# A hybrid attention block on one core: the first 256 channels in tiles of 128, the root in column form

## Chip, cores and metric

One core of a Trainium2 chip runs the whole block in one launch. The metric is device time in microseconds of one execution, as the median of several runs; a profile of one execution gives its span, from the first to the last instruction.

## The reference

One layer over 512 latent tokens and 256 context tokens of width 2048. Both streams are normalised and modulated, projected by one matrix, and pass through two groups of four heads (gated linear attention and mLSTM, in both directions); then an output projection, a convolutional SwiGLU and a final norm. What matters here is its beginning:

```python
mod = (c_act @ w_mod + b_mod)[:, None, :]         # c_act = silu(c)
mod_c = (cc_act @ w_mod + b_mod)[None, None, :]   # cc_act = silu(c_ctx)
sh1, sc1, gt1, sh2, sc2, gt2 = jnp.split(mod, 6, axis=-1)
csh1, csc1, cgt1, csh2, csc2, cgt2 = jnp.split(mod_c, 6, axis=-1)
h  = rmsnorm(x, g_norm1) * (1 + sc1) + sh1        # x: 512 tokens x 2048
hc = rmsnorm(ctx, g_norm1) * (1 + csc1) + csh1    # ctx: 256 tokens x 2048
z  = jnp.einsum('btd,dp->btp', h, w_in)           # q, k, v, gates of all heads
```

`rmsnorm` divides each token by the root of the mean square of its 2048 channels. All arrays are float32.

## The kernel before, in words

Tokens lie along the free dimension and channels on the 128 partitions, so x is sixteen tiles `xl[k]` of 128 channels x 512 tokens; the context is `xc[k]`, 128 x 256, two to a transfer (`xcp`). Every product of activations and weights is made in three passes: each operand is split into a high part (ACT rounds it) and a low part (DVE subtracts), and `mm3` adds high x high, high x low and low x high. `load_split` fetches a 512 KB piece of weights, two channel tiles by 512 columns (q 128, k 128, v 256 of one head), and splits it.

The head of the program is `project_first` (line 411). Its TensorE instructions are pinned: `mm` and `tr` keep them in the order in which they are written. It projects heads 0 and 1, pair of channel tiles by pair (`kp`, eight of them). Head 0 has six accumulators that stay in PSUM for all pairs (`banks`, groups g: 0 is q, 1 is k, 2 and 3 are v of the latent, 4 and 5 are k and v of the context). Head 1 is made one pair at a time in two other banks (`early_group`) and added to sums in SBUF.

Ahead of the first product stand:

- 16 transfers of x on SP's queue, and with each of the first 14 a filler product into an idle bank (line 418), whose result nothing uses.
- `stream_rstd` (line 539): ACT squares each tile, DVE adds the sixteen squares to one, and TensorE multiplies by ones, which gives every partition the sum of a token's squares; `mean_rsqrt` then makes the root on all 128 x 512 elements (`rl`).
- `mod_load`, `mod_rows`, `mod_cols` (lines 273 to 309), for region 1 (scale) and region 0 (shift) and 256 channels each: four pieces of 512 KB are fetched, sixteen products with the activated conditioning (`cact`) as the stationary side give rows, ACT copies them, two transposes and a reduction on DVE turn them into columns `scol` and `shcol`.
- `modulate(n, streams)` (line 562), for two channel tiles: DVE multiplies x by scale and root, ACT adds the shift into the high part `hTh`, DVE makes the low part `hTl`.

The same steps for later pairs are laid between products, so that their waits run under them. The context is squared, summed, rooted (`ss_c`) and modulated after the first products of head 1; `shifted` leaves h itself in the tiles of x for a later product. In the loop over `kp`, head 1's six groups come first, then head 0's, with the rows of the next pairs among them.

Two things set the order of the rest: instructions under `tc.high_priority()` go ahead of others on their engine, and `tc.issue_after(ins)` keeps a block's instructions behind one. SP issues transfers in program order, and one that has to wait for a buffer holds back those behind it. The buffers named `raw` are seven for scale and shift (`mraw`) and four for weights (`wraw`); the fourth piece of every scale or shift load goes into `wraw`. PSUM has six banks for accumulators (`acc`) and two for the rest (`psb`).

Of the kernel before, what the change touches and what calls it, by code (L numbers as in the profile page):

```python
# [11 lines left out]
F32 = mybir.dt.float32  # L12
F32R = mybir.dt.float32r
# [5 lines left out]
P = 128  # L19
# [65 lines left out]
def block_kernel(ctx: ExitStack, tc: tile.TileContext, a: dict, out: bass.AP):  # L85
# [25 lines left out]
    def mm(*args, **kw):  # L111
        ins = PE.matmul(*args, **kw)  # L112
        if pinned[0]:
            tc.keep_in_program_order(ins)
# [43 lines left out]
    def acc(name, shape=(P, T)):  # L158
        return (banks8[0] if banks8 else psA).tile(list(shape), F32, name=name, tag="acc")
# [113 lines left out]
    def mod_load(region, n):  # L273

        raws = []
        for q in range(4):
            raws.append((wraw if q == 3 else mraw).tile([P, 4, 256], F32, name=f"raw_m{region}_{n}_{q}", tag="raw"))
            nc.sync.dma_start(raws[q], a["w_mod1"][8 * region + n, q])
        return raws

    def mod_rows(region, n, raws):

        bank = psb(f"ps_m{region}_{n}")
        ps = bank[:, 0:256]
        for q in range(4):
            for g in range(4):
                mm(ps[32 * g : 32 * g + 32, :], cact[:, 4 * q + g, :], raws[q][:, g, :],
                   start=(q == 0), stop=(q == 3), skip_group_check=True)
        rows = tmp.tile([P, 256], F32, name=f"rows_m{region}_{n}", tag="rows")
        with tc.high_priority():  # L290
            S.copy(rows, ps)
        return bank, rows
# [115 lines left out]

    early_both = []

    def project_first():

        banks = [acc(f"a0_{g}", BANKS[g]) for g in range(6)]
# [12 lines left out]
        with tc.high_priority():  # L426
            ins = modulate(0, "x")

        for _ in range(6):
            mm(banks[5][:, 0:P], ones, rl[:, 0:P], start=True, stop=True)  # L430
        early_pair(w1, sums)
        for g in range(2, 4):
            early_group(0, g, w1, sums)
        project_chunk(0, *w0, banks[0], 0)
        rows = mod_rows(1, 1, raws[1])
        project_chunk(0, *w0, banks[1], 1)
        mod_cols(1, 1, *rows)
        with tc.high_priority(), tc.issue_after(ins):
            stream_rstd([x.rearrange("p a b -> p (a b)") for x in xcp], rc, "c", TC)
            ins = modulate(0, "c")  # L440
        for g in range(2, 4):
            project_chunk(0, *w0, banks[g], g)
        rows = mod_rows(0, 1, raws[0])
        early_group(0, 4, w1, sums)
        mod_cols(0, 1, *rows)
        early_group(0, 5, w1, sums)
        with tc.issue_after(ins):
            modulate(1, "xc")
        w1 = load_split(a["w_heads"][1, 1], f"h1_1")
        for r in (1, 0):  # L450
            raws[r] = mod_load(r, 2)
        nc.sync.dma_start(cst[:, 0:C_ID], a["consts"][:, 0:C_ID])
        project_chunk(0, *w0, banks[4], 4)
        rows = mod_rows(1, 2, raws[1])
        project_chunk(0, *w0, banks[5], 5)
        mod_cols(1, 2, *rows)
        shifted(0)
        for kp in range(1, KP):
            for g in range(6):
                if g == 5 and kp + 1 < KP:  # L460
                    rows = mod_rows(0, kp + 1, raws[0])
                ins = early_group(kp, g, w1, sums)
                if g == 2:
                    with tc.issue_after(ins):
                        w0 = load_split(a["w_heads"][0, kp], f"h0_{kp}")
                    if kp + 2 < KP:
                        raws[1] = mod_load(1, kp + 2)
            if kp + 1 < KP:
                mod_cols(0, kp + 1, *rows)
                with tc.issue_after(ins):  # L470
                    modulate(kp + 1, "xc")
# [47 lines left out]
    rstd = xp.tile([P, T + TC], F32, name="rstd")  # L519

    nc.sync.dma_start(cv, a["cvec"])
    xl = [ytile(k, f"xl{k}") for k in range(KT)]
    xcp = [actp.tile([P, 2, TC], F32, name=f"xc{j}", tag=f"al{KT // 2 + j}") for j in range(KT // 2)]
    xc = [xcp[k // 2][:, k % 2, :] for k in range(KT)]
    for k in range(KT):
        nc.sync.dma_start(xl[k], a["xT"][k])
    nc.sync.dma_start(cst[:, C_ID : C_LO + 2], a["consts"][:, C_ID : C_LO + 2])
# [8 lines left out]

    V.tensor_scalar(out=bp1, in0=bmod[:, 16:32], scalar1=1.0, scalar2=None, op0=ALU.add)

    def stream_rstd(xs, o, name, n):

        tot = xp.tile([P, T], F32, name=f"sq_{name}", tag="sqs")
        for k, x in enumerate(xs):
            if k == 0:
                sq = tot
            elif len(xs) == KT:
                tag = f"ah{1 + k}" if k < 11 else f"al{k - 9}"
                sq = actp.tile([P, T], F32, name=f"sq_{name}{k}", tag=tag)
            else:
                sq = tmp.tile([P, T], F32, name=f"sq_{name}{k}", tag="sq")
            S.activation(sq, x, AF.Square)  # L550
            if k:
                add(tot, tot, sq)
        ps = psb(f"ss_{name}", (P, n))
# [4 lines left out]
        mean_rsqrt(ps, D, var, scr, o)  # L558

    rl, rc = rstd[:, 0:T], rstd[:, T:]  # L560

    def modulate(n, streams):
        def part(x, r, k, c, hi, lo):
            S.activation(hi, x, AF.Identity, bias=shcol[:, k, c : c + 1])
            return V.scalar_tensor_tensor(out=lo, in0=x, scalar=shcol[:, k, c : c + 1], in1=hi.bitcast(F32), op0=ALU.add,
                                          op1=ALU.subtract).ins

        ks = (2 * n, 2 * n + 1)
        for k in ks:
            if "x" in streams:  # L570
                V.scalar_tensor_tensor(out=xl[k], in0=xl[k], scalar=scol[:, k, 0:1], in1=rl, op0=ALU.mult, op1=ALU.mult)
            if "c" in streams:
                V.scalar_tensor_tensor(out=xc[k], in0=xc[k], scalar=scol[:, k, 1:2], in1=rc, op0=ALU.mult, op1=ALU.mult)
# [911 lines left out]
def arrange(x, c, ctx, c_ctx, w_mod, b_mod, g_norm1, g_norm2, w_in, gla_w_lr, gla_b_lr, mlstm_b_gate,  # L1485
# [18 lines left out]
    r["xT"] = x[0].T.reshape(KT, P, T)  # L1504
    r["ctxT"] = ctx[0].T.reshape(KT // 2, 2, P, TC).transpose(0, 2, 1, 3)
    r["w_mod1"] = w_mod[0][:, : 2 * D].reshape(4, 4, P, 16, 256).transpose(3, 0, 2, 1, 4)
    r["w_mod2"] = w_mod[0][:, 2 * D :].T.reshape(4, KT, P, 2, 2, T).transpose(3, 0, 1, 2, 4, 5)
    small = np.concatenate([w_in[:, GLA_COLS["lr"] : GLA_COLS["lr"] + 16], w_in[:, ML_COLS["lr"] : ML_COLS["lr"] + 16]], 1)
    r["w_small"] = small.reshape(KT, P, 32).transpose(1, 0, 2)
# [43 lines left out]
```

## Time and profile before

| | us |
|---|---|
| median of 3 runs | 2439.01 (2438.06 to 2441.04) |
| the profiled execution | 2438.32 |
| its span | 2436.3 |
| TensorE busy | 2410.7 (99%) |
| VectorE busy | 1784.9 (73%) |
| ScalarE busy | 1016.7 (42%) |

The profile gives busy time by engine and by group of instructions, a timeline in which neighbouring instructions of a kind are merged, and for each idle stretch the engine or transfer that ended it. PE is TensorE's products and PEld its weight loads. A float32 product that isn't split into parts runs as two passes, and each pass has a record of its own. A product's record includes its latency, so records overlap: the pace of a series is read from the distance of its starts.

### The profile page before, as it was taken

Reading aid. Unit: us, or ns where it says so; the run is one execution under the profiler, and the core shown is the slowest. Engines: PE = TensorE matmul, PEld = TensorE weight load, DVE = VectorE, ACT = ScalarE, POOL = GpSimd, SP = SyncE. Lnnn points to the kernel's source line nnn. Section 1 sums busy time; section 2 is a strip of 40 time slices with the busy share of each in tenths; the row PEclk is TensorE's granted clock in tenths of the full one; section 3 lists DMA queues with packets and bytes.
Section 4 is the critical chain, followed back from the end, with each engine's and each line's share of the span. In section 5 each row is a group of like instructions: output and inputs, shape, how many; then the busy total and the mean of one; then the engine's idle time right before and its main releaser. Section 6 shows DMA issues by size and latency. Waiting matters only on the chain.

```text
span 2436.3 us, 38579 instructions
## 1 busy us (share of the span) xinstructions
PE 2410.7 (99%) x15402; PEld 2169.3 (89%) x15402; DVE 1784.9 (73%) x2848; ACT 1016.7 (42%) x1510; POOL 176.1 (7%) x221
## 2 busy tenths in 40 slices
PE   8999999999999999999999999999999999999998
PEld 5888899899988888888898989898989999999997
DVE  6567866555456586779987888878787878787886
ACT  5235533322233232246544444444444444444445
POOL 0000000000000000000202010101010111111021
PEclk9999999999999999999999999999999999999999
DMA  9751111233355797833646464645555555546464
GB/s 389 283 182 48 45 53 52 70 127 116 129 196 192 229 329 274 289 123 108 151 127 160 113 152 122 145 124 143 134 131 143 133 140 124 145 123 154 114 187 133
DMA packets 122485, 373.61 MB, mean 153 GB/s; under 512 B 13912, under 2 KB 19010, under 8 KB 122306
## 3 DMA queue, kind: packets, MB, share of 16 engines
q1 hardware_dynamic: 95298, 318.71, 39.9%
q0 software_dynamic: 25920, 51.40, 11.6%
q8 instruction: 120, 1.97, 0.3%
q10 hardware_dynamic: 1088, 1.05, 0.1%
q14 instruction: 59, 0.48, 0.1%
HBM read 320.77 MB, written 50.34 MB: 152 GB/s over the span
## 4 chain that ended last, share of the span: by engine, by line
PE 83%; issue 9%; DVE 4%; DMA 2%; ACT 1%; POOL 0%; SPq 0%; POOLq 0%; DVEq 0%; ACTq 0%
PE a L112 18%; PE uv L112 17%; PE dn L112 15%; PE ug L112 15%; PE ga L112 7%; PE wo L112 3%; PE po L112 2%; PE ps_m L112 1%; DVE cv L1307 1%; PE sl L112 1%; DMA raw_uv<-in_w_up 1%; PE st L112 1%; PE cst L112 1%; DVE lo_d L107 1%; DVE ex L95 0%
## 5 line engine op out<-in xcount | busy, mean ns | idle before, releaser
L112 PE MATMUL dn<-gh,lo_d 128*128 128x512 f32 x672 | 262.3, 390 | 0.6 <-DVE lo_d L107 0.4
L112 PE MATMUL dn<-gh,hi_d 128*128 128x512 f32 x672 | 261.7, 389 | 0.0
L112 PE MATMUL dn<-gl,hi_d 128*128 128x512 f32 x672 | 261.6, 389 | 0.0
L1307 DVE SCALAR_TENSOR_TENSOR cv<-pads,cwt,cv 128x512 f32<-128x512 f32 x344 | 238.8, 744 | 0.6
L1361 POOL DMA_DIRECT2D x2d<-st x160 | 140.1, 933 | 1140.7 <-ACT st L1360 1071.4
L107 DVE TENSOR_TENSOR lo_buv<-sum_uv,hi_buv 128x1024 fp32r<-128x1024 f32 x80 | 97.9, 1224 | 104.0 <-ACT hi_buv L106 101.8
L325 DVE SCALAR_TENSOR_TENSOR raw_m<-raw_m,crow 128x1024 f32<-128x1024 f32 x128 | 154.6, 1229 | 1.4 <-DMA raw_m<-in_w_mod 1.4
L112 PEld LDWEIGHTS dn<-gh,lo_d 128*128 128x128 f32 x672 | 126.1, 188 | 29.3 <-DVE lo_d L107 3.2
L112 PE MATMUL a<-hi_h,hTh 128*128 128x256 f32 x512 | 151.8, 296 | 0.5 <-ACT e L407 0.5
L112 PEld LDWEIGHTS dn<-gl,hi_d 128*128 128x128 f32 x672 | 126.2, 188 | 25.9
L112 PEld LDWEIGHTS dn<-gh,hi_d 128*128 128x128 f32 x672 | 126.2, 188 | 25.6
L112 PE MATMUL a<-lo_h,hTh 128*128 128x256 f32 x512 | 144.7, 283 | 0.0
L112 PE MATMUL a<-hi_h,hTl 128*128 128x256 f32 x512 | 144.7, 283 | 0.0
L106 ACT CAST hi_d<-raw_d 128x1024 fp32r<-128x1024 f32 x86 | 88.6, 1030 | 132.3 <-PE ug L112 70.6
L107 DVE TENSOR_TENSOR lo_d<-raw_d,hi_d 128x1024 fp32r<-128x1024 f32 x86 | 102.7, 1195 | 48.8 <-ACT hi_d L106 48.1
L112 PE MATMUL ug<-bth,hi_bug 128*128 128x256 f32 x480 | 136.8, 285 | 0.2 <-DVE t L1326 0.2
L112 PE MATMUL uv<-bqh,lo_auv 128*128 128x256 f32 x480 | 135.9, 283 | 0.0
L112 PE MATMUL ug<-bqh,lo_aug 128*128 128x256 f32 x480 | 135.8, 283 | 0.0
L112 PE MATMUL uv<-bth,lo_buv 128*128 128x256 f32 x480 | 135.8, 283 | 0.0
L112 PE MATMUL uv<-bql,hi_auv 128*128 128x256 f32 x480 | 135.8, 283 | 0.0
L112 PE MATMUL uv<-btl,hi_buv 128*128 128x256 f32 x480 | 135.8, 283 | 0.0
L112 PE MATMUL uv<-bth,hi_buv 128*128 128x256 f32 x480 | 135.8, 283 | 0.0
(415 smaller groups left out, 7256.4 us busy)
## 6 DMA issues: line engine op xcount, KB each, us to landing
raw_m<-in_w_mod SPq DMA_DIRECT2D x192, 512.0 KB, 5.2
raw_d<-in_w_down SPq DMA_DIRECT2D x82, 512.0 KB, 3.5
raw_ug<-in_w_up SPq DMA_DIRECT2D x80, 512.0 KB, 3.5
x2d<-st POOLq DMA_DIRECT2D x160, 256.0 KB, 5.4
raw_uv<-in_w_up SPq DMA_DIRECT2D x80, 512.0 KB, 5.4
raw_h<-in_w_heads SPq DMA_DIRECT2D x64, 512.0 KB, 3.5
raw_ga<-in_w_gates SPq DMA_DIRECT2D x32, 512.0 KB, 3.6
raw_wo<-in_w_out SPq DMA_DIRECT2D x32, 512.0 KB, 4.6
```

Of the source, the lines that this page charges most:

```text
L106: cast[0] = S.copy(hi, x).ins
L107: return V.tensor_tensor(out=lo, in0=x, in1=hi.bitcast(F32), op=ALU.subtract).ins
L112: ins = PE.matmul(*args, **kw)
L325: V.scalar_tensor_tensor(out=x, in0=x, scalar=1.0, in1=crow[0], op0=ALU.mult, op1=ALU.mult, accum_out=mtot[:, at : at + 1])
L1307: V.scalar_tensor_tensor(out=t3, in0=src, scalar=w, in1=t3, op0=ALU.mult, op1=ALU.add)
L1361: nc.gpsimd.dma_start(x2d[k], t, accum_op=ALU.add)
```

## The change

The first two channel tiles are treated one at a time, each in steps of 128 channels:

- Scale and shift of a tile are fetched as two pieces of 512 KB each (`tile_load`, from a new arrangement `w_mod0` of the same weights), and made by `tile_rows` and `tile_cols` with 128 columns and one transpose.
- One 512 KB piece holds one channel tile of the weights of both heads 0 and 1 (`first_weights`, split in two halves by `first_split`).
- `first_tile` makes, for one channel tile, q and k of both heads and v of head 0, into six banks (`banks[0..3]` and two for head 1, `q1`). Head 1's v follows after the second tile; the context groups of both heads follow after that, when `q1` has been copied out and its banks are free.
- The order of transfers becomes: scale and shift of tile 0, weights of tile 0, scale and shift of tile 1, weights of tile 1, context, and then the rows of the next pairs.
- `root_first` sums the squares of x on two engines: DVE adds tiles 0, 2, 4, ... 12 and TensorE multiplies that sum and the nine other squares by a column of ones, 128 tokens at a time, into 128 x 4 sums. The root is made on 128 x 4 elements, spread over the partitions by four products with the identity, and copied to SBUF. The fillers are 256 columns wide instead of 384, and three more stand under the root.
- The column of ones is fetched ahead of x by a transfer of its own.
- The context's squares are issued in two parts, after the modulation of tile 1; its root comes after head 1's v.
- For `kp` = 1 the loop is written out with another placing of the row steps and of the weight loads; from `kp` = 2 on the old loop runs. `modulate` takes a list of tiles.

The core of the diff:

```diff
+    def tile_rows(region, t, raws):
+        bank = psb(f"ps_t{region}_{t}")
+        ps = bank[:, 0:P]
+        for q in range(4):
+            for g in range(4):
+                k = 4 * q + g
+                mm(ps[32 * g : 32 * g + 32, :], cact[:, k, :], raws[k // KP][:, k % KP, :],
+                   start=(q == 0), stop=(q == 3), skip_group_check=True)
...
+    def first_tile(kk, w, o4, q1):
+        wh, wl = w
+        for n, (ws, xs) in enumerate(((wh, hx[0]), (wl, hx[0]), (wh, hx[1]))):
+            for head, o in ((0, o4[0:2]), (1, q1)):
+                for g in range(2):
+                    mm(o[g], ws[:, head, P * g : P * g + P], xs[kk], start=(n == 0 and kk == 0),
+                       stop=(n == 2 and kk == 1 and head == 1))
+        for g in range(2, 4):
+            for b in range(2):
+                js = slice(P * (2 * g - 4 + b), P * (2 * g - 3 + b))
+                mm3(o4[g][:, b, :], hx[0][kk][:, js], hx[1][kk][:, js], wh[:, 0, 256:], wl[:, 0, 256:],
+                    kk == 0 and b == 0, False, skip_group_check=True)
...
     def project_first():
...
-        for k in range(14):
-            mm(banks[5], xl[k][:, 0:P], xl[k][:, 0 : DK + DV], start=True, stop=True)
-        stream_rstd(xl, rl, "l", T)
-        for r in (1, 0):
-            mod_cols(r, 0, *mod_rows(r, 0, mod_load(r, 0)))
-        w1, w0 = (load_split(a["w_heads"][h, 0], f"h{h}_0") for h in (1, 0))
+        root_first(q1[1])
+        raws = {(r, t): tile_load(r, t) for r, t in ((1, 0), (0, 0))}
+        raw0 = first_weights(0)
+        raws.update({(r, t): tile_load(r, t) for r, t in ((1, 1), (0, 1))})
+        raw1 = first_weights(1)
         for j in range(KT // 2):
             nc.sync.dma_start(xcp[j], a["ctxT"][j])
+        for r in (1, 0):
+            tile_cols(r, 0, *tile_rows(r, 0, raws[r, 0]))
+        with tc.high_priority():
+            modulate((0,), "x")
+        w0 = first_split(0, raw0)
+        for _ in range(6):
+            mm(q1[1][:, 0:P], ones, rl[:, 0:P], start=True, stop=True)
+        first_tile(0, w0, banks, q1)
+        for r in (1, 0):
+            tile_cols(r, 1, *tile_rows(r, 1, raws[r, 1]))
+        w1 = first_split(1, raw1)
+        with tc.high_priority():
+            ins = modulate((1,), "x")
+        squares_c = squares([x.rearrange("p a b -> p (a b)") for x in xcp], "c")
+        with tc.high_priority(), tc.issue_after(ins):
+            next(squares_c)
         raws = {r: mod_load(r, 1) for r in (1, 0)}
...
+        first_tile(1, w1, banks, q1)
...
         for g in range(2, 4):
+            early_group(0, g, heads[1], sums)
+        with tc.high_priority(), tc.issue_after(ins):
+            root(tot_c, rc, "c", TC)
+            ins = modulate((0, 1), "c")
         rows = mod_rows(1, 1, raws[1])
         mod_cols(1, 1, *rows)
+        banks += [acc(f"a0_{g}", BANKS[g]) for g in (4, 5)]
+        early_group(0, 4, heads[1], sums)
+        early_group(0, 5, heads[1], sums)
+        for g in (4, 5):
+            project_chunk(0, *heads[0], banks[g], g)
+        mod_cols(0, 1, *mod_rows(0, 1, raws[0]))
         with tc.issue_after(ins):
-            modulate(1, "xc")
+            modulate((2, 3), "xc")
...
+        shifted(0)
+        for g in range(6):
+            ins = early_group(1, g, w1, sums)
...
+    def root_first(idle):
+        tot = xp.tile([P, T], F32, name="sq_l0", tag="sqs")
+        ps = psb("ss_l", (P, TJ))
+        own = (1, 3, 5, 7, 9, 11, 13, 14, 15)
+        order = (1, 3, 5, 7, 9, 11, 13, 0, 14, 15)
...
+        for k in range(KT):
+            if k < 14:
+                mm(idle[:, 0:256], xl[k][:, 0:P], xl[k][:, 0:256], start=True, stop=True)
+            done = order[(k - 3) // 2] if k in (3, 5, 7, 9, 11, 13) else None
+            for n in ([done] if done else order[6:] if k == KT - 1 else ()):
+                for j in range(TJ):
+                    mm(ps[:, j : j + 1], sqs[n][:, P * j : P * j + P], cst[:, C_ONE : C_ONE + 1],
+                       start=(n == order[0] and j == 0), stop=(n == order[-1]), skip_group_check=True)
+        var, scr, r = (xp.tile([P, TJ], F32, name=f"{t}_l", tag=t) for t in ("var4", "scr4", "r4"))
+        with tc.high_priority():
+            mean_rsqrt(ps, D, var, scr, r)
+        for n in range(3):
+            mm(idle[:, 0:256], xl[15][:, 0:P], xl[15][:, 0:256], start=True, stop=True)
+        o = psb("rb_l")
+        for j in range(TJ):
+            mm(o[:, P * j : P * j + P], r[:, j : j + 1].to_broadcast([P, P]), ident, start=True, stop=True)
+        with tc.high_priority():
+            S.copy(rl, o)
```

More of the change, by code (lines that the diff above doesn't have):

```diff
@@ L409, in block_kernel, with tile_load @@
     early_both = []
+    def tile_load(region, t):
+        raws = [mraw.tile([P, KP, P], F32, name=f"raw_t{region}_{t}_{i}", tag="raw") for i in range(2)]
+        for i in range(2):
+            nc.sync.dma_start(raws[i], a["w_mod0"][region, t, i])
+        return raws
+    def tile_rows(region, t, raws):
[6 more added lines that the diff above has]
+                   start=(q == 0), stop=(q == 3), skip_group_check=True)
+        rows = tmp.tile([P, P], F32, name=f"rows_t{region}_{t}", tag="rows")
+        with tc.high_priority():
+            S.copy(rows, ps)
+        return bank, rows
@@ new lines, in tile_cols @@
+    def tile_cols(region, t, bank, rows):
+        pt = bank[:, 256 : 256 + P]
+        tr(pt, rows, ident)
+        o = (scol if region == 1 else shcol)[:, t, :]
+        with tc.high_priority():
+            V.tensor_reduce(out=o, in_=pt.rearrange("p (g c) -> p c g", g=4)[:, 0:2, :], axis=mybir.AxisListType.X, op=ALU.add)
+            if region == 1:
+                V.tensor_scalar(out=o, in0=o, scalar1=bp1[:, t : t + 1], scalar2=gn1[:, t : t + 1], op0=ALU.add, op1=ALU.mult)
+            else:
+                V.tensor_scalar(out=o, in0=o, scalar1=bmod[:, t : t + 1], scalar2=None, op0=ALU.add)
@@ new lines, in block_kernel, with __init__, __getitem__, first_weights @@
+    class HeadRows:
+        def __init__(self, tiles, head):
+            self.tiles, self.head = tiles, head
+        def __getitem__(self, at):
+            return self.tiles[at[1]][:, self.head, at[2]]
+    def first_weights(kk):
+        raw = wraw.tile([P, 2, 512], F32, name=f"raw_w{kk}", tag="raw")
+        nc.sync.dma_start(raw, a["w_heads"][0:2, 0, :, kk, :].rearrange("h p c -> p h c"))
+        return raw
+    def first_split(kk, raw):
+        hi = whi.tile([P, 2, 512], F32R, name=f"hi_w{kk}", tag="hi1")
+        lo = wlo.tile([P, 2, 512], F32R, name=f"lo_w{kk}", tag="lo1")
+        with tc.high_priority():
+            for c in (slice(0, 256), slice(256, 512)):
+                parted[0] = split(hi[:, :, c], lo[:, :, c], raw[:, :, c])
+        return hi, lo
@@ L411, in project_first @@
     def project_first():
-        banks = [acc(f"a0_{g}", BANKS[g]) for g in range(6)]
+        q1 = [acc(f"a1_0_{g}") for g in range(2)]
+        banks = [acc(f"a0_{g}", BANKS[g]) for g in range(4)]
         both = accp.tile([P, CJ, T], F32, name="e0_c", tag="sums")
@@ new lines, in project_first @@
+        first_tile(0, w0, banks, q1)
+        for r in (1, 0):
+            tile_cols(r, 1, *tile_rows(r, 1, raws[r, 1]))
+        w1 = first_split(1, raw1)
+        with tc.high_priority():
+            ins = modulate((1,), "x")
+        squares_c = squares([x.rearrange("p a b -> p (a b)") for x in xcp], "c")
+        with tc.high_priority(), tc.issue_after(ins):
+            next(squares_c)
+        raws = {r: mod_load(r, 1) for r in (1, 0)}
+        first_tile(1, w1, banks, q1)
+        for g in range(2):
+            sums[g] = actp.tile(list(BANKS[g]), F32, name=f"e0_{g}", tag=f"ah{KT - 4 + g}")
+            with tc.high_priority():
+                tc.keep_in_program_order(S.activation(sums[g], q1[g], AF.Copy, scale=SCALE if g == 0 else 1.0))
@@ L426, in project_first @@
         with tc.high_priority():
[L427 to L431, printed above, removed]
+            tot_c = next(squares_c)
+        heads = [[HeadRows([w0[part], w1[part]], head) for part in range(2)] for head in range(2)]
         for g in range(2, 4):
-            early_group(0, g, w1, sums)
-        project_chunk(0, *w0, banks[0], 0)
+            early_group(0, g, heads[1], sums)
@@ L452, in project_first @@
         nc.sync.dma_start(cst[:, 0:C_ID], a["consts"][:, 0:C_ID])
-        project_chunk(0, *w0, banks[4], 4)
-        rows = mod_rows(1, 2, raws[1])
-        project_chunk(0, *w0, banks[5], 5)
-        mod_cols(1, 2, *rows)
-        shifted(0)
-        for kp in range(1, KP):
+        shifted(0)
+        for g in range(6):
+            ins = early_group(1, g, w1, sums)
+            if g == 2:
+                with tc.high_priority(), tc.issue_after(ins):
+                    w0 = split_new(w0, "h0_1", (2, 512))
+                raws[1, 3] = mod_load(1, 3)
+            if g == 4:
+                rows = mod_rows(1, 2, raws[1])
+        mod_cols(1, 2, *rows)
+        shifted(1)
+        for g in range(6):
+            project_chunk(1, *w0, banks[g], g)
+            if g == 0:
+                rows = mod_rows(0, 2, raws[0])
+            if g == 1:
+                mod_cols(0, 2, *rows)
+                modulate((4, 5), "xc")
+            if g == 2:
+                w1 = load_split(a["w_heads"][1, 2], f"h1_2")
+                raws[0] = mod_load(0, 3)
+            if g == 4:
+                rows = mod_rows(1, 3, raws[1, 3])
+        mod_cols(1, 3, *rows)
+        for kp in range(2, KP):
             for g in range(6):
```

50 lines of the change are left out of this document (26 added, 24 removed).

## The prediction

> **What bounds the kernel now.** I read the page's totals first, then the slices, then the timeline of TensorE (PE) over the first 80 us, then its neighbours on VectorE (DVE), ScalarE (ACT) and the queue SP.
>
> ```profile
> span 2436.3 us, 38579 instructions
> PE 2410.7 (99%) x15402; PEld 2169.3 (89%) x15402; DVE 1784.9 (73%) x2848; ACT 1016.7 (42%) x1510; POOL 176.1 (7%) x221
> ```
>
> PE is busy 99% of the span. The change touches the first 75 us, where PE has an empty head and a few gaps, so the question is how late the first product starts and how many gaps follow. In the next rows the columns are start, length, engine, line, operation, and in brackets the idle time before it and who ended it.
>
> ```profile
> 3.98 10.94 PE L112 MATMUL a<-xl 128*128 128x384 f32 x28 [3.98 <-DMA xl<-in_xT]
> 18.04 2.08 PE L112 MATMUL ss_l<-sq_l,cst 128*128 128x512 f32 x2 [3.12 <-DVE sq_l L101]
> 20.05 3.64 PE L112 MATMUL ps_m<-raw_m,cact 128*32 128x256 f32 x32
> 24.55 1.93 PE L112 MATMUL ps_m<-raw_m,cact 128*32 128x256 f32 x32
> 26.98 0.44 PE L117 MATMUL ps_m<-cst,rows_m 128*128 128x128 f32 x2 [0.49 <-ACT rows_m L291]
> 28.74 1.34 PE L112 MATMUL a<-hTh,hi_h 128*128 128x512 f32 x4
> 32.38 0.39 PE L112 MATMUL a<-hi_h,hTh 128*128 128x256 f32 x1 [0.46 <-ACT e L407]
> 39.04 0.64 PE L112 MATMUL ps_m<-raw_m,cact 128*32 128x256 f32 x8 [0.62 <-DMA raw_m<-in_w_mod]
> 48.91 0.45 PE L112 MATMUL a<-hi_h,hch 128*128 128x384 f32 x1 [0.36 <-ACT e_c L393]
> 54.68 0.44 PE L117 MATMUL ps_m<-cst,rows_m 128*128 128x128 f32 x2 [0.30 <-ACT rows_m L291]
> 54.88 0.48 PE L112 MATMUL a<-hTh,hi_h 128*128 128x512 f32 x1
> 55.19 0.39 PE L112 MATMUL a<-hTl,hi_h 128*128 128x512 f32 x1
> 55.42 0.39 PE L112 MATMUL a<-hTh,lo_h 128*128 128x512 f32 x1
> ```
>
> Fillers, then the sum of squares at 18.04, the scale and shift rows for 256 channels, and the first product at 28.74. From there PE waits only 0.46, 0.62, 0.36 and 0.30: 1.74 us up to 54.88, where the second pair of channel tiles (kp=1) begins. So a gain must come from the 28.74, and anything that the change puts uncovered between products is paid in full.
>
> The transfers are full over the head:
>
> ```profile
> 10.00:20.00 10.00, 6.88 (x18) 2.77 (x16) 7.01 (x11) 5.72 (x10) 0.00 (x0) 0.87 1.05 413
> 25.81 0.20 PEld L112 LDWEIGHTS ps_m<-raw_m,cact 128*32 128x32 f32 x8 [0.23 <-DMA raw_m<-in_w_mod]
> 0.82 0.39 SPq L521 DMA_DIRECT2D cv<-in_cvec  x1
> 1.27 9.16 SPq L526 DMA_DIRECT2D xl<-in_xT  x16
> ```
>
> 413 GB/s (last column): a 512 KB piece takes 1.27 us. The shift weights are complete at 25.8.
>
> **The change, step by step.**
>
> *Transfers.* Two tiles of 128 channels (1 MB for scale, 1 MB for shift) replace 4 MB ahead of the first weights. One small constants transfer goes ahead of xl and moves it 0.45 us (0.82 to 1.27 is one issue). Two MB less: the first shift tile lands at 25.8 - 5.1 + 0.45 = 21.2, the first weights at 22.5, the second pair of tiles by 27.6, its weights by 28.8. Bytes in all are the same. There are eight tile pieces for seven buffers, so SP holds the eighth (and the weights, ctx and later rows behind it) until the first tile is used, near 24.9 below. Seven pieces ahead of it cover that; it lands near 30 and is used at 36. I cost the queue at nothing; without that cover it is the issue-to-landing time of one piece, 5 us. POOL's queue is not passed.
>
> *Squares.* DVE keeps seven additions instead of fifteen. PE takes the other nine and the sum: ten tiles x four 128x1 products, each two passes in f32 as the x28 for 14 fillers shows, so 80 passes, plus 28 passes of 256 columns for the fillers. The same column form stands at the end of this kernel:
>
> ```profile
> 1067.31 2.75 PEld L112 LDWEIGHTS ps_rms<-cst,sqsq 128*128 128x128 f32 x24 [0.60 <-PE wo L112]
> 1069.99 0.75 PEld L112 LDWEIGHTS rb_rms<-sqsq,cst 128*128 128x128 f32 x6
> 1071.33 1.09 PEld L112 LDWEIGHTS rb_rms<-cst,rs_rms 128*128 128x128 f32 x8 [0.60 <-DVE rs_rms L180]
> ...
> 41.32 1.03 PE L112 MATMUL ss_c<-sq_c,cst 128*128 128x256 f32 x4
> L112 PE MATMUL ss_c<-sq_c,cst x4: 379/380/381, 41.3 to 42.0; 128*128 128x256 f32 x4
> ...
> 6.70 0.34 PEld L112 LDWEIGHTS a<-xl 128*128 128x128 f32 x1 [0.30 <-issue]
> 7.26 1.80 PEld L112 LDWEIGHTS a<-xl 128*128 128x128 f32 x6 [0.22 <-issue]
> 9.47 6.46 ACT L550 ACTIVATE sq_l<-xl 128x512 f32<-128x512 f32 x10 [0.85 <-DMA xl<-in_xT]
> ```
>
> A column pass costs its weight load: (1069.99 - 1067.31) / 24 = 0.112 us. A 256-column pass is (1.03 - 0.38) / 3 = 0.22. So PE has 80 x 0.112 + 28 x 0.22 = 9.0 + 6.1 = 15.1 us of work at full clock, starting at 3.98 + 0.45 = 4.4. The loads of 0.34 us up to 6.70 (0.19 later) show half clock for the first 3.4 us, which costs 1.7 more: end at 21.2. The squares themselves are done on ACT at 15.93 + 0.45 = 16.4, so the sum is now held by PE, not by DVE or the transfers. Bounds: 17.3 if the passes keep up and only the last tile's eight (0.9) remain after 16.4; 22.9 if half clock lasts twice as long. I take 21.2, since the passes are priced by the same operation. Before, the sum's last pass ended at 20.1.
>
> *Root in column form.* From the last column pass to the broadcast products 1071.33 - 1069.99 = 1.34, and 1.1 for the eight of them: the first scale rows start at 23.65. The copy of rl to SBUF runs on ACT beside them.
>
> *Scale and shift of tile 0.* The row pass is half as wide. 32 passes took 1.93 us at 256 columns; half is 1.0, unchanged is 1.9, and I take 1.3, nearest to the pace of the weight loads (24 in 1.02, next fence). Rows 23.65 to 24.95, 0.5 for the copy (idle of 0.49 above), transpose 0.15, shift rows 25.6 to 26.9, copy 0.5, transpose at 27.4. From transpose to product took 28.74 - 26.98 = 1.76, less 0.1 for one transpose fewer: first product at 29.05. **+0.3 us.** The halved loads gain nothing, because PE's own sum arrives later than they do.
>
> *Tile 1.* Its rows stood before 28.74; now they stand between first_tile(0) and first_tile(1), pinned in program order with nothing to run under their waits: rows 1.3, copy 0.5, transpose 0.15, rows 1.3, copy 0.5, then 1.66 to the product. **+5.4 us.** The product work is equal: two heads, two tiles, same widths. Bounds 4.8 and 6.6 by the row price.
>
> *Context root.*
>
> ```profile
> 24.55 1.02 PEld L112 LDWEIGHTS ps_m<-raw_m,cact 128*32 128x32 f32 x24 [0.17 <-issue]
> 42.39 0.47 ACT L175 ACTIVATE scr_c<-ss_c,eps 128x256 f32<-128x256 f32 x1 [2.27 <-PE ss_c L112]
> 45.24 0.91 ACT L564 ACTIVATE hch<-xc,shcol 128x256 fp32r<-128x256 f32 x2 [1.93 <-DVE xc L573]
> 45.78 0.89 DVE L565 SCALAR_TENSOR_TENSOR hcl<-xc,shcol,hch 128x256 fp32r<-128x256 f32 x2 [0.18 <-ACT hch L564]
> 45.15 1.93 PE L112 MATMUL ps_m<-raw_m,cact 128*32 128x256 f32 x32
> ```
>
> From the end of ss_c (42.35) to the last hcl (46.67) are 4.3 us. Before, 2.8 us of products (42.35 to 45.15) and the 1.9 us row pass lay under it; now only one row pass and its transpose do. That leaves a copy wait of 0.5 and about 1.0 before early_group(0, 4) runs free. The eight context squares follow the modulation of tile 1 on ACT and are added by the time the products of head 1 end. **+1.5**, bounds 0 and 2.5.
>
> *Start of kp=1.* mod_cols(0, 1) now stands directly ahead of early_group(1, 0), which needs channels 2 and 3. Before, its rows (45.15) lay ten us ahead of 54.88. Now: 0.5 for the copy, then 1.66 less the 0.25 transpose to the first product, and the remaining parts arrive one by one:
>
> ```profile
> 66.35 0.73 ACT L564 ACTIVATE hTh<-xl,shcol 128x512 fp32r<-128x512 f32 x1 [2.25 <-DVE shcol L101]
> 67.41 0.72 ACT L564 ACTIVATE hTh<-xl,shcol 128x512 fp32r<-128x512 f32 x1
> 68.75 0.75 DVE L565 SCALAR_TENSOR_TENSOR hTl<-xl,shcol,hTh 128x512 fp32r<-128x512 f32 x1
> ```
>
> The last low part ends 2.4 us after the first high part (67.08 to 69.50), against 1.4 us of products in the group: 0.9 more. **+2.8**, bounds 1.5 and 4.
>
> *What goes.* The four gaps, 1.74, and some 0.4 in the first twelve products (28.74 to 32.38 less the 0.46, against 2.8 at the 0.23 between 55.19 and 55.42), where the low part came late. **-2.1.** Eviction of q1 stays under the products; row loads of kp=1 land before their turn; from kp=2 on the code is the old loop.
>
> Sum: 0.3 + 5.4 + 1.5 + 2.8 - 2.1 = **+7.9 us** on the profiled execution of 2438.32 (2 us round its span), which is 0.7 below the median 2439.01. Later stages are paced by PE, so the delay passes through: 2446.9.
>
> The Trainium skill, "TensorE: Matmul & The Clock Gate", Part 1, says that the clock opens after one busy window of some 3.4 us, and that the windows run freely, so a start inside a window can cost a further one. The trace agrees in size (half clock from 3.98 to about 7.1 here).
>
> **Rivals.**
>
> *A: the column passes keep up with the arrivals.* The sum then ends at 17.3, the first product at 25.15, 3.9 earlier: +4.0, 2443.0. The 0.112 per pass speaks against it.
>
> *B: half clock lasts another 3.4 us.* At half speed that puts off 1.7 us of work: +9.6, 2448.6. The clock column shows that it can happen:
>
> ```profile
> 16.00:18.00 2.00, 0.00 (x0) 0.00 (x0) 1.79 (x4) 0.00 (x0) 0.00 (x0) 0.85 1.02 418
> 20.00:22.00 2.00, 2.00 (x21) 0.97 (x24) 1.12 (x2) 1.32 (x2) 0.00 (x0) 0.50 1.02 416
> 24.00:26.00 2.00, 1.82 (x30) 1.08 (x34) 1.23 (x5) 0.12 (x1) 0.00 (x0) 0.94 1.02 418
> ```
>
> Half clock stayed from about 17.4 to 24.1, though PE was busy from 18.04 on. Against it: after 4.4 PE is never idle.
>
> *C: faster, the head rides on the transfers.* 2.6 MB less ahead of the first product is 6.3 us at 413 GB/s, so a product at 22.4 and, if tile 1 is made ready beside products, 2432.7. For it: PE waited on a piece at 25.81. Against it: by the steps above a product at 22.4 needs the sum done at 14.6, before the squares are (16.4), and the gain is over 0.2% only from a product at 23.8 (sum done at 16.0) on; the waits of tile 1 would have to vanish too, which the pinned order forbids.
>
> *D: no difference.* The waits at the context root and at kp=1 are mostly covered and slack later takes the rest: +3 at most, 2442.0. Gaps of a few tenths after 54.88 leave little slack.
>
> **How the numbers follow.** Main 0.60, A 0.17, B 0.12, C 0.04, D 0.07. The main case's own range is 2443.5 to 2450, from the row price (1.8 less to 1.8 more) and the two covered waits. 0.2% is 4.9 us, about what a measurement of this kernel can tell from no change. Slower: B and nearly all of main, 0.69. Same: A, D and the low edge of main, 0.27. Faster 0.04. The range 2441.5 to 2450.5 takes in A, main and B, and leaves out C and half of D.
>
> **What would show it.** The last ss_l pass near 21 with PE unbroken from 4.4; the first product near 29; some 5.4 us between the two blocks of first products; a PE wait of over 1 us ahead of the first product of kp=1 near 59; kp=2 starting some 8 us later than before. A last ss_l pass near 17, or no wait ahead of first_tile(1), would make it wrong.

## The result

The changed kernel takes 2462.07 us in the median of 6 runs (2448.99 to 2463.56), the kernel before 2439.02 in 6 runs beside them (2437.53 to 2441.04). The ratio is 1.0083, 95% interval 1.0069 to 1.0097; it is lower than that of the medians (1.0095), as two of the six runs, 2448.99 and 2454.55, lie well below the other four. It is slower, as forecast, but by 23 us, where 7.9 was the number and 11.5 the upper end of the range. The profiled execution took 2461.86. From its page, the totals and the clock row:

```profile
span 2460.2 us, 38895 instructions
PE 2431.8 (99%) x15558; PEld 2193.4 (89%) x15558; DVE 1777.8 (72%) x2844; ACT 1017.0 (41%) x1515; POOL 176.6 (7%) x221
PEclk9999999999999999999999999999999999999999
```

The span is 23.9 us longer and PE is busy 21.1 us longer (2431.8 against 2410.7). So most of the loss is not waiting: PE is "busy" more. The clock row tells nothing. PE's timeline of the changed kernel tells more (start, length, operation, count, and the idle time before it):

```profile
4.35 2.07 PE L112 MATMUL a<-xl 128*128 128x256 f32 x4 [4.35 <-DMA xl<-in_xT]
7.00 2.07 PE L112 MATMUL a<-xl 128*128 128x256 f32 x4 [0.59 <-DMA xl<-in_xT]
8.87 1.71 PE L112 MATMUL ss_l<-cst,sq_l 128*128 128x1 f32 x8
10.44 2.05 PE L112 MATMUL a<-xl 128*128 128x256 f32 x4
...
25.94 8.53 PE L112 MATMUL ss_l<-cst,sq_l 128*128 128x1 f32 x40
34.33 2.91 PE L112 MATMUL a<-xl 128*128 128x256 f32 x6
37.03 1.39 PE L112 MATMUL rb_l<-cst,r_l 128*128 128x128 f32 x8
38.35 1.08 PE L112 MATMUL ps_t<-raw_t,cact 128*32 128x128 f32 x32
43.15 1.19 PE L112 MATMUL a<-hTh,hi_w 128*128 128x512 f32 x4
47.52 1.08 PE L112 MATMUL ps_t<-raw_t,cact 128*32 128x128 f32 x32
...
52.86 1.20 PE L112 MATMUL a<-hTh,hi_w 128*128 128x512 f32 x4 [1.81 <-ACT hTh L704]
63.52 0.44 PE L117 MATMUL ps_m<-cst,rows_m 128*128 128x128 f32 x2 [0.49 <-ACT rows_m L291]
64.65 0.44 PE L112 MATMUL a<-hi_w,hch 128*128 128x384 f32 x1 [0.70 <-ACT hch L704]
71.90 0.44 PE L117 MATMUL ps_m<-cst,rows_m 128*128 128x128 f32 x2 [0.49 <-ACT rows_m L291]
73.62 0.50 PE L112 MATMUL a<-hTh,hi_h 128*128 128x512 f32 x1 [1.29 <-ACT hTh L704]
74.41 0.50 PE L112 MATMUL a<-hTl,hi_h 128*128 128x512 f32 x1 [0.28 <-DVE hTl L707]
98.50 0.48 PE L112 MATMUL a<-hTh,hi_h 128*128 128x512 f32 x1
```

A column pass takes 8.53 / 40 = 0.213 us, not 0.112, and four 256-column filler passes take 1.87 (7.00 to 8.87), not 0.9. All of PE's work from 4.35 to about 37.7 runs at half clock: 33 us, not 3.4. At 38.35 the row passes run at full speed (32 in 1.08). The sum of squares ends at 34.3 instead of 21.2, and the first product stands at 43.15 instead of 28.74: 14.4 us of the loss. The pair kp=2 begins at 98.50; in the kernel before it began here:

```profile
74.96 0.40 PE L112 MATMUL a<-hTh,hi_h 128*128 128x512 f32 x1
```

That is 23.54 us, and the span is 23.9 us longer: practically all of it arises before kp=2. There is one more stretch at half clock, which the table of windows does show (window, its length, busy time of PE, PEld, DVE, ACT and POOL, granted clock, DMA share, GB/s):

```profile
30.00:40.00 10.00, 9.61 (x68) 8.64 (x68) 0.65 (x4) 1.32 (x4) 0.00 (x0) 1.00 0.00 0
70.00:74.00 4.00, 2.22 (x31) 0.97 (x23) 1.96 (x4) 2.57 (x6) 0.00 (x0) 1.00 0.71 243
74.00:76.00 2.00, 1.62 (x5) 0.99 (x5) 1.81 (x4) 2.00 (x4) 0.00 (x0) 0.81 0.88 290
76.00:78.00 2.00, 2.00 (x6) 1.57 (x5) 0.69 (x1) 0.21 (x1) 0.00 (x0) 0.50 1.02 407
78.00:80.00 2.00, 2.00 (x13) 1.76 (x13) 0.69 (x1) 0.00 (x0) 0.00 (x0) 0.83 0.22 88
```

After the waits ahead of kp=1 (PE busy 2.22 of 4 us) the clock falls to 0.50 for 3.41 us (75.26 to 78.67 by the trace's records of the clock), which costs about 1.6. Note the first line: the granted clock reads 1.00 in a stretch in which the passes have half speed until 37.7. The column follows changes that the trace records. The first record of this run is the change to full clock at 37.71; before it the column stands at 1.00.

### The profile page after: what moved, and what is told of

It reads as the page before. It is cut to its first block, busy times and chain, and to the rows that moved or that the text cites. A ratio compares the mean times of both kernels' runs of the same rounds, so it can differ in the third digit from the quotient of the medians.

```text
span 2460.2 us, 38895 instructions
## 1 busy us (share of the span) xinstructions
PE 2431.8 (99%) x15558; PEld 2193.4 (89%) x15558; DVE 1777.8 (72%) x2844; ACT 1017.0 (41%) x1515; POOL 176.6 (7%) x221
## 4 chain that ended last, share of the span: by engine, by line
PE 84%; issue 10%; DVE 4%; ACT 1%; DMA 1%; POOL 1%; SPq 0%; POOLq 0%; ACTq 0%; DVEq 0%
PE a L112 19%; PE dn L112 16%; PE uv L112 16%; PE ug L112 15%; PE ga L112 7%; PE wo L112 3%; PE po L112 2%; PE ps_m L112 1%; PE sl L112 1%; PE st L112 1%; PE ss_l L112 1%; PE cst L112 1%; DVE cv L1448 0%; DVE ex L95 0%; POOL x2d L1502 0%
## 5 line engine op out<-in xcount | busy, mean ns | idle before, releaser
L112 PE MATMUL ug<-bth,lo_bug 128*128 128x256 f32 x480 | 135.8, 283 | 0.0
L112 PE MATMUL ug<-bqh,hi_aug 128*128 128x256 f32 x480 | 135.8, 283 | 0.0
```

## Experiments

The theory: the narrow passes of the new root do not count as work for the clock, so it stays shut; all other terms of the change are as forecast. The rival: column passes are simply slower than the 0.112 priced, whatever the clock, or the new order of the transfers does it.

**The start alone** (`root_only`): the kernel before, with the new root, the transfer of its column of ones ahead of x, and nothing else of the change.

```diff
-        for k in range(14):
-            mm(banks[5], xl[k][:, 0:P], xl[k][:, 0 : DK + DV], start=True, stop=True)
-        stream_rstd(xl, rl, "l", T)
+        root_first(banks[5])
...
```

> The kernel before with only the new sum and root of x (nine squares by TensorE in column form, fillers of 256 columns). Theory: the column passes between the fillers leave TensorE at half clock until the sum is done near 34 us, as in the profile of the changed kernel; then the rows of 256 channels and the first product near 45 instead of 28.7, nothing else changes: about 2455 us, with single runs near 2442 where the clock opens early. Rival (the delay comes from the tiles, their buffers and the stopped transfers, not from the sum): within 3 us of 2439.

Measured: 2455.03 (2445.55, 2454.89, 2455.17, 2455.23), ratio 1.0064, interval 1.0047 to 1.0081. One program has two times, 9.5 us apart, as the changed kernel has. The profiled execution is the short one (near 2442 was expected for such a run). Its PE timeline:

```profile
4.40 4.04 PE L112 MATMUL a<-xl 128*128 128x256 f32 x8 [4.40 <-DMA xl<-in_xT]
17.05 4.52 PE L112 MATMUL ss_l<-cst,sq_l 128*128 128x1 f32 x40
21.44 2.65 PE L112 MATMUL a<-xl 128*128 128x256 f32 x6
23.88 1.65 PE L112 MATMUL rb_l<-cst,r_l 128*128 128x128 f32 x8
32.41 1.34 PE L112 MATMUL a<-hTh,hi_h 128*128 128x512 f32 x4
```

Here the eight first filler passes ran without the 0.59 us wait, and the clock opened at 8.06, just ahead of the first column pass (8.27). A column pass takes 4.52 / 40 = 0.113, and the sum ends near 21.5: the 21.2 of the prediction. But then the fillers and the broadcast are slow again (2.65 and 1.65; by the prediction's prices at full clock 1.3 and 1.1): with 40 column passes one after the other, 4.5 us, the clock that was open fell, at 21.72. So the price per pass was right, and the clock was not. That the executions near 2455 are those in which the clock stayed shut was not profiled; the 9.5 us are only of a size with it (the changed kernel's sum ends 13.1 us late).

**The tiles alone** (`tiles_only`): the changed kernel with the root and the fillers of before.

```diff
-        root_first(q1[1])
+        for k in range(14):
+            mm(q1[1][:, 0:384], xl[k][:, 0:P], xl[k][:, 0:384], start=True, stop=True)
+        stream_rstd(xl, rl, "l", T)
...
```

> The changed kernel with the old sum and root of x (fillers of 384 columns, fifteen additions on VectorE, row form) in place of the new ones; tiles, order of transfers and the written-out second pair of tiles stay. Theory: the clock opens near 7 us as before, the sum ends near 20.6 and the first product comes near 26.9; the uncovered waits of tile 1, of the context and of kp=1 remain: +5.7 us, 2443 to 2447, and runs that agree within 3 us. Rival (the tiles hold up the start by themselves): 2455 or more.

Measured: 2445.57 in 9 runs (2440.51 to 2447.26), ratio 1.0024, interval 1.0014 to 1.0034. The median is within what was expected; the runs spread over 6.8 us, where 3 was expected. PE's timeline:

```profile
25.44 1.19 PE L112 MATMUL a<-hTh,hi_w 128*128 128x512 f32 x4 [0.68 <-ACT hTh L727]
35.16 2.08 PE L112 MATMUL a<-hTh,hi_w 128*128 128x512 f32 x4 [1.81 <-ACT hTh L727]
49.63 0.44 PE L112 MATMUL a<-hi_w,hch 128*128 128x384 f32 x1 [0.66 <-ACT hch L727]
58.57 0.50 PE L112 MATMUL a<-hTh,hi_h 128*128 128x512 f32 x1 [1.28 <-ACT hTh L727]
```

The first product comes 3.3 us earlier than in the kernel before (25.44 against 28.74), so neither the tiles nor the new order of the transfers holds up the start. The kernel is 6 us slower all the same, a quarter of the change's 23 us. The waits behind the first product are the changed kernel's to 0.05 us. But the second line shows more than a wait: its four products take 2.08 us, where the changed kernel's took 1.20. Here the clock fell with the wait of tile 1 and stayed at 0.50 from 34.48 to 41.31, which costs about 3.1 us. The pair kp=2 begins at 81.91, 6.95 later than before; without the lost clock it would be some 3.9.

**A burst ahead of x** (`warm_start`): the changed kernel with three products of 512 columns on a constant tile before its fillers.

```diff
+        for _ in range(3):
+            mm(idle, warm[:, 0:P], warm, start=True, stop=True)
...
```

> The changed kernel with three products of 512 columns on a constant tile ahead of the first filler, from about 1.6 us on, results unused. Theory (the clock does not open because too little streaming falls into a window at the start; once open it stays open, since the sum then runs at 0.112 a pass): sum done near 22, first product near 30, 2446 to 2449, no run above 2451. Rival (the column passes also let an open clock fall back): weight loads of 0.3 us again among the column passes and 2455 to 2463. Rival (the column passes are slow for another reason than the clock): as the changed kernel, plus up to 2.

Measured: 2450.45 (2448.32 to 2453.18), ratio 1.0046, interval 1.0031 to 1.0061. PE's timeline:

```profile
1.56 4.25 PE L112 MATMUL a<-warm 128*128 128x512 f32 x6 [1.56 <-DVE warm L641]
17.38 4.78 PE L112 MATMUL ss_l<-cst,sq_l 128*128 128x1 f32 x40
22.02 2.91 PE L112 MATMUL a<-xl 128*128 128x256 f32 x6
30.59 1.20 PE L112 MATMUL a<-hTh,hi_w 128*128 128x512 f32 x4
```

Added work of 4 us takes nearly 12 us off the changed kernel's median. Nothing else differs, so the clock is shown as the cause: the first product moves from 43.15 to 30.59. It also holds through the mixed stretch (fillers and column passes by turns) and falls again at 21.50, under the 40 column passes: the six filler passes behind them take 2.91, at half clock. It falls once more at kp=1 (0.50 from 62.45 to 65.87). The profiled execution, 2448.32, has these losses and still lies in the 2446 to 2449 expected. The median is 1.5 us above it, and two runs, 2452.05 and 2453.18, lie above the 2451 that none was to exceed; no trace shows what they lost.

**Wider fillers** (`wide_fill`): the changed kernel with 512 columns in each filler instead of 256, so twice the filler work.

```diff
-                mm(idle[:, 0:256], xl[k][:, 0:P], xl[k][:, 0:256], start=True, stop=True)
+                mm(idle, xl[k][:, 0:P], xl[k], start=True, stop=True)
```

> The changed kernel with fillers of 512 columns instead of 256, so that streamed columns fill 67% instead of 50% of TensorE's time at half clock. Theory (too small a share of streamed columns in a window keeps the clock shut): the clock opens within some 10 us in most runs, sum near 27, first product near 35, about 2453 us: faster than the changed kernel although TensorE gets more work. Rival (column passes keep the clock shut whatever lies between them): half clock until the sum near 45, first product near 54, about 2473 us.

Measured: 2458.43 (2457.93 to 2460.07), ratio 1.0082, interval 1.0068 to 1.0095. PE's timeline:

```profile
4.58 5.26 PE L112 MATMUL a<-xl 128*128 128x512 f32 x8 [4.58 <-DMA xl<-in_xT]
22.73 4.52 PE L112 MATMUL ss_l<-cst,sq_l 128*128 128x1 f32 x40
27.11 1.82 PE L112 MATMUL a<-xl 128*128 128x256 f32 x6
28.73 1.92 PE L112 MATMUL rb_l<-cst,r_l 128*128 128x128 f32 x8
```

With more to do, PE ends the sum 7 us sooner (27.2 against 34.3), because the passes run at 0.113. That is what the theory says and the rival excludes. The time lies 5.4 us above what the theory gave, and 3.6 below the changed kernel. The clock fell three more times in the profiled execution, each time for 3.41 us: behind the columns at 28.24 (`rb_l` 1.92 instead of 1.1), at tile 1's wait at 45.31, and at kp=1's waits at 69.20. The four runs lie within 2.1 us, where the changed kernel's six spread over 14.6; that the clock opened early in all four would explain it, but only one was profiled.

**All squares on VectorE** (`vector_sum`): the column form for the finished sum alone, 8 column passes instead of 80.

```diff
-        own = (1, 3, 5, 7, 9, 11, 13, 14, 15)
-        order = (1, 3, 5, 7, 9, 11, 13, 0, 14, 15)
+        own = ()
+        order = (0,)
...
```

> The changed kernel with all squares summed on VectorE and only the sum in column form (8 passes instead of 80); fillers stay 256 columns wide. Theory: without column passes between them even the narrow fillers stream without a break and open the clock near 8 us; sum near 18.5, first product 27 to 29, 2444 to 2448. Rival (the narrower fillers alone keep the clock shut): weight loads of 0.3 us up to 15 us; since TensorE then has little to do, 2446 to 2450, so the weight loads decide, not the time.

Measured: 2450.66 (2444.65 to 2452.20), ratio 1.0041, interval 1.0026 to 1.0056. PE's timeline:

```profile
7.08 8.54 PE L112 MATMUL a<-xl 128*128 128x256 f32 x24 [0.68 <-DMA xl<-in_xT]
19.19 1.87 PE L112 MATMUL ss_l<-cst,sq_l 128*128 128x1 f32 x8 [3.57 <-DVE sq_l L101]
20.92 2.91 PE L112 MATMUL a<-xl 128*128 128x256 f32 x6
29.95 1.20 PE L112 MATMUL a<-hTh,hi_w 128*128 128x512 f32 x4
...
9.05 0.50 PEld L112 LDWEIGHTS a<-xl 128*128 128x128 f32 x2 [0.62 <-DMA xl<-in_xT]
12.34 0.30 PEld L112 LDWEIGHTS a<-xl 128*128 128x128 f32 x2 [0.27 <-DMA xl<-in_xT]
```

It missed the expected 2444 to 2448 by 2.7, and the first product came at 29.95, not 27 to 29: now PE is idle for 3.57 us before the sum, and the eight passes (0.23 each) and the root behind them run at half clock. A wait and a stretch of column passes have the same effect on the clock.

The weight loads in the last two lines answer the rival. The start is the changed kernel's: the same 256-column fillers, and a wait of 0.68 after the first four passes. With no column passes between them the clock opens, at 11.09 (a pair of loads takes 0.50 before and 0.30 behind it); it is later than the 8 expected, but narrow fillers alone do not keep it shut. In the changed kernel, with column passes from 8.87 on, it stayed shut until 37.71.

**The kernel before, kept streaming** (`before_held`): five fillers more, so that PE streams until the sum is there.

```diff
-        for k in range(14):
+        for k in [*range(KT), KT - 1, KT - 1, KT - 1]:
```

> The kernel before with five more fillers of 384 columns, so that TensorE streams until the squares are summed and the clock stays open past 18 us. Theory (the head of the kernel before waits for its second transfer of rows at 25.8, not for TensorE): row passes run at full clock, the first product stays near 28.7, within 1.5 us of 2439. Rival (the half clock from 17 to 24 us costs what it lasts): 2 to 3 us faster.

Measured: 2438.94 in 11 runs (2437.10 to 2440.32), ratio 1.0001, interval 0.9992 to 1.001. Its half clock from 17 to 24 us, which the prediction quoted, cost nothing. PE's timeline says why:

```profile
24.52 0.64 PE L112 MATMUL ps_m<-raw_m,cact 128*32 128x256 f32 x8 [0.55 <-DMA raw_m<-in_w_mod]
25.74 0.64 PE L112 MATMUL ps_m<-raw_m,cact 128*32 128x256 f32 x8 [0.58 <-DMA raw_m<-in_w_mod]
```

With the clock open the row pass waits for its pieces instead: the head of the kernel before rides on the transfers.

**The waits laid under products** (`covered`): `tiles_only` with the burst and more fillers, tile 1's rows and transposes put between the passes of `first_tile(0)`, the context root one group earlier, and the shift rows of kp=1 between the context groups.

```diff
-        first_tile(0, w0, banks, q1)
-        for r in (1, 0):
-            tile_cols(r, 1, *tile_rows(r, 1, raws[r, 1]))
+        steps = first_tile(0, w0, banks, q1)
+        next(steps)
+        rows = tile_rows(1, 1, raws[1, 1])
+        next(steps)
+        tile_cols(1, 1, *rows)
...
-        for g in range(2, 4):
-            early_group(0, g, heads[1], sums)
+        early_group(0, 2, heads[1], sums)
         with tc.high_priority(), tc.issue_after(ins):
             root(tot_c, rc, "c", TC)
```

> The changed kernel with the old sum and root in row form, a warm start of three constant products, fillers until the sum, and the waits laid under products: tile 1's rows and transposes between the passes of first_tile(0), the context's root between head 1's two v groups, and the shift rows of channels 2 and 3 ahead of the context groups. Theory (what the tiles cost is the uncovered waits, 5.4 + 1.5 + 2.8 us by the prediction's terms, of which 2.4 + 0.6 + 2.1 can be covered): first product near 25.4, kp=2 some 2 us earlier than before, 2435.5 to 2438.5. Rival (the tiles cost by their extra instructions or transfers, not by waits): 2442 to 2446, as with the old root alone.

Measured: 2441.33 in 11 runs (2438.72 to 2443.35), ratio 1.0009, interval 1.0000 to 1.0018; the expected 2435.5 to 2438.5 was missed. PE's timeline:

```profile
39.68 1.10 PE L112 MATMUL ss_c<-sq_c,cst 128*128 128x256 f32 x4 [1.31 <-DVE sq_c L101]
44.89 0.44 PE L117 MATMUL ps_m<-cst,rows_m 128*128 128x128 f32 x2 [0.82 <-ACT rows_m L291]
52.95 0.50 PE L112 MATMUL a<-hTh,hi_h 128*128 128x512 f32 x1 [1.14 <-ACT hi_h L106]
54.22 0.50 PE L112 MATMUL a<-hTh,lo_h 128*128 128x512 f32 x1 [0.53 <-DVE lo_h L107]
```

The waits of tile 1 and of the context's `hch` are gone, and others stand in their place: the context's squares are not added yet, and the weights of kp=1 are split late. Once open, the clock does not fall in the head, and kp=2 begins 1.21 later than before. The span is 2.97 longer. The other 1.8 fits the clock near 1070 us, which stands at 0.50 for 6.83 us here and for 3.41 in the kernel before.

**Tile 1 uncovered again** (`tile_bare`): `covered`, but with tile 1's rows between the two blocks, as in the change.

```diff
-        next(steps)
-        rows = tile_rows(1, 1, raws[1, 1])
...
+        for _ in steps:
+            pass
+        for r in (1, 0):
+            tile_cols(r, 1, *tile_rows(r, 1, raws[r, 1]))
```

> As covered, but tile 1's rows and transposes stand between the two first_tile blocks again, as in the changed kernel. Theory: the two copies (0.4 each) and the wait for the modulated tile (1.7) come back: 2.3 us more than covered. Rival (transfers hold tile 1 anyway): the same time as covered.

Measured: 2444.97 in 10 runs (2442.65 to 2446.41), ratio 1.0023, interval 1.0014 to 1.0032: 3.6 us more than `covered`, against the 2.3 expected. The wait that comes back is this one, after two of 0.39:

```profile
35.47 2.08 PE L112 MATMUL a<-hTh,hi_w 128*128 128x512 f32 x4 [1.81 <-ACT hTh L735]
```

The three waits sum to 2.6, and kp=2 begins 3.4 us later by the trace. The line shows the rest: its four products take 2.08 us instead of 1.20, because the clock is at 0.50 from 35.24 to 38.66. That costs about 1.6, while the wait for the context's squares shrinks by 1.1 (from 1.31 to 0.21). So what the copies and the wait cost by themselves was expected about rightly, and a lost clock was not reckoned with.

**The remaining waits taken away by order** (`covered2`): `covered`, with the context root after both groups, the two row passes together, and the weights of kp=1 split ahead of the modulation.

```diff
+        rows1 = mod_rows(1, 1, raws[1])
+        rows = mod_rows(0, 1, raws[0])
+        mod_cols(1, 1, *rows1)
...
+        w1 = load_split(a["w_heads"][1, 1], f"h1_1")
         for g in (4, 5):
             project_chunk(0, *heads[0], banks[g], g)
         with tc.issue_after(ins):
             modulate((2, 3), "xc")
-        w1 = load_split(a["w_heads"][1, 1], f"h1_1")
```

> The covered kernel with its three remaining waits taken away by order alone: the context's sum of squares after both of head 1's remaining groups (1.31 us of wait in covered), both row passes of the second pair of channel tiles one after the other so that the copy of the first runs under the second (0.82), and the weights of kp=1 split ahead of the modulation that they shared ACT and DVE with (1.14 and 0.53). Theory (after the clock, what the change costs are these waits and nothing else): 3.8 us at most come off 2441.3, so 2437.5 to 2439.0, level with before or just under it, with no PE wait above 0.6 us between the first product and kp=2. Rival (the waits are moved, since the modulation of kp=1's tiles now comes after the split on the same engines): 2440.5 to 2442, with a wait of 1.5 us or more ahead of kp=1 on hTh or hTl.

Measured: 2439.09 in 11 runs (2437.18 to 2442.31), beside 2439.91 of the kernel before; ratio 0.9999, interval 0.999 to 1.0008: 0.1 above the theory's range, below the rival's, and level with the kernel before. PE's timeline:

```profile
44.68 0.64 PE L112 MATMUL ps_m<-raw_m,cact 128*32 128x256 f32 x8 [0.57 <-DMA raw_m<-in_w_mod]
51.92 0.50 PE L112 MATMUL a<-hTh,hi_h 128*128 128x512 f32 x1 [0.61 <-ACT hi_h L106]
```

Its first product stands at 25.30, 3.4 us ahead of the kernel before, and its kp=2 0.18 behind it; the clock reads 1.00 from the first product to there. The lead goes to tile 1's two row passes, some 2 us that now lie behind the first product instead of ahead of it, and to waits, none above 0.61 (the two largest are shown). The remainder was not followed. Of all kernels run, none is faster than the kernel before.

## Why the prediction was right and wrong

*The step that failed* is the sum of squares: "half clock for the first 3.4 us, which costs 1.7 more: end at 21.2", and with it the first product at 29.05 and the term +0.3, which measured +14.41. The work was counted and priced rightly: `root_only` with the clock open ends the sum at 21.5, with 0.113 a pass. The time of the gate (the change to full clock) was taken from the kernel before, where PE streams 384 columns in every pass. In the changed kernel the first fillers are narrower and are cut by a wait of 0.59 at 6.4, and from 8.87 on half of the time is column passes. Then the clock stayed shut until 3.4 us after the last of them. The root took 4.0 instead of 2.45 as its six filler passes were at half clock (34.3 to 38.35), and the rows were 0.6 quicker than priced (32 passes in 1.08, not 1.3, and shorter waits for the copies): 13.1 + 1.55 - 0.6 = 14.1 on top of the 0.3.

*Rival B* was that mechanism, and "after 4.4 PE is never idle" was the wrong reason against it: PE was hardly idle, and that did not open the clock. Its price, one more 3.4 us, was about a tenth of the 33 us at half clock that came.

The Trainium skill, "TensorE: Matmul & The Clock Gate", Part 1, says that the warm-up budget is some 3.4 us of time and not a number of matmuls. The trace disagrees for these passes: PE had matmuls running from 7.00 to 37 with no wait, at half clock. It agrees for wide ones: the clock opened 2.9 us after the first of the 512-column passes in `warm_start`, 3.2 in `wide_fill`. The Trainium skill, in the same part of that page, also says that an idle window of that length shuts the clock. It fell with 4.5 us of column passes alone, in `root_only`, `warm_start` and `wide_fill`, which fits if such passes count as idle. But it also fell behind single waits of no more than 1.81 us (`tiles_only`, `tile_bare`, `wide_fill`), which are shorter.

*Tile 1*, +5.4: 52.86 - 47.52 = 5.34. The waits are the ones named; that the size fits so closely is partly luck. Rows and copies took 0.66 less than priced (1.47 twice, not 1.8), and from the second transpose to the product it took 2.14, not 1.66.

*Context root*, +1.5: 0.49 + 0.70 = 1.19. Right, within its bounds.

*Start of kp=1*, +2.8: waits of 0.49, 1.29 and 0.28, and some 0.5 to 0.8 in late parts, so 2.6 to 2.9. Right; that the clock would drop behind these waits for 3.4 us was not foreseen, and added 1.6. A drop does not follow from a wait with certainty. Behind kp=1's waits the clock fell in the changed kernel, `warm_start`, `vector_sum` and `wide_fill`, and not in `tiles_only`. Behind tile 1's it fell in `tiles_only`, `tile_bare` and `wide_fill`, and not in the changed kernel, `warm_start` and `vector_sum`. The waits are the same to 0.05 us.

*What goes*, -2.1: right. None of the four gaps of the kernel before is left, and the first twelve products take 2.85 us (43.15 to 46.00).

*The queue at nothing*: SP did stick on the eighth piece, and longer than forecast, as its buffer came free with the late rows:

```profile
15.82 23.56 SPq L415 DMA_DIRECT2D raw_t<-in_w_mod  x4
39.43 0.43 SPq L455 DMA_DIRECT2D raw_w<-in_w_heads  x1
```

The transfers then stand at 0 GB/s from 30 to 40 us. Yet no PE wait of the changed kernel on a transfer follows, as nothing behind it was due: the cover held.

*The sum*: 7.9 forecast, + 14.1 for the clock at the start, + 1.6 for that at kp=1, gives 23.6; kp=2 starts 23.54 later. The size was wrong through the clock, in two places, of which the first is nine tenths. Without the root the change costs 6.2 by the medians (`tiles_only`, with 2439.39 for the kernel before beside it). About half of that is a drop of the clock too, in the profiled execution, but kp=2 would start some 3.9 late without it, so the direction does not hang on the clock.

What stays open is how the share of wide passes sets the gate; only 256 and 512 columns were tried beside column passes. The traces give a hint, which no run was made to test. In every profiled run the times between recorded changes in the first 100 us are whole multiples of 3.413 us. In the 3.413 us that ended with the opening PE streamed 1792 columns in `root_only` and `vector_sum`, 1920 in the kernel before and `tiles_only`, and 2048 in `warm_start` and `wide_fill`; in the changed kernel, while the clock was shut, it was never more than 1032 in such a stretch until the column passes had ended. One stretch does not fit without more: in `tiles_only` 1920 columns with 0.65 us of idle time did not open it.

Open as well are some 1 to 5 us that several kernels lose late. In `root_only` kp=2 starts 2.8 late and the span is 7.5 longer; part of it is a wait of 1.30 at 1223 us that the kernel before lacks. In `covered` and `vector_sum` some 1.7 of it would be the clock: near 1070 to 1080 us they stand at 0.50 for 6.83 us, the kernel before for 3.41.

## What to carry to other kernels

By these traces a matmul of one column keeps TensorE busy in the profile and does not open or hold its clock: put such passes in after the clock has opened on wide ones, and in short runs with wide passes between (8 of them, 0.95 us, did not shut an open clock here; 40 of them, 4.5 us, did). Check the clock by the length of equal passes, not by the clock column alone. Price a clock's warm-up from the passes that will run in it, not from those that they replace. Beside the length of an uncovered wait, reckon with the half clock that can follow it: here 1.6 to 3.1 us behind waits of about 2 us, in some runs and not in others. Where a head rides on its transfers, fewer bytes ahead of the first product buy an earlier start only: if the products behind it wait for the same bytes, or for steps that were hidden before, the lead is given back.

## What the runs showed of the hardware

- A pass of one column costs 0.113 us at full clock (40 in 4.52) and 0.213 at half (40 in 8.53); it scales with the clock.
- Such passes do not keep the clock open: after 4.5 us of them alone, four fillers of 256 columns had taken 1.11 us and the next six took 2.91 (`warm_start`).
- Mixed by halves with fillers of 256 columns, they let an open clock stay open (`warm_start`, 8.6 to 17.4) but did not let a shut one open (the changed kernel, 8.9 to 25.9). Without them the same fillers opened it (`vector_sum`, at 11.09). That would explain why one program runs in two times, 2445.55 and 2455, 2448.99 and 2462; only one execution of each was profiled.
- The stretches at half clock behind a wait or a run of column passes last 3.41 or 6.83 us in all of these traces, up to 100 us. A wait of 1.81 us, with two of 0.39 ahead of it, was enough in three runs (`tiles_only`, `tile_bare`, `wide_fill`) and not in three others.
- The granted clock reads 1.00 until its first recorded change, also where every pass has half speed (the changed kernel, until 37.71).
